# A mixture-of-experts stage on one Trainium2 core: other runs per weight load, a gather of four experts in rounded halves, a split scatter

## The chip, the cores and the metric

The kernel runs on one core of a Trainium2 chip. The core has a matrix engine (TensorE, PE, with its weight loads shown apart as PEld), a vector engine (VectorE, DVE), an engine for pointwise functions (ScalarE, ACT), a general engine (GpSimd, POOL) and a sync engine (SyncE, SP) that issues most of the transfers from memory. The metric is the device time of one execution in microseconds. Three runs of the kernel before took 1729.75, 1730.45 and 1731.28 us; the median is 1730.45.

## The reference

Two blocks of two layers each work on 256 tokens of 1024 numbers. Both layers of the second block end in a mixture of experts, and this is all that the change touches:

```python
def hierarchical_moe(x, w_group, b_group, w_expert, b_expert, w_gate, w_up, w_down):
    ...
    combine = jnp.sum(jax.nn.one_hot(expert_id, N_EXPERTS, dtype=jnp.float32) * top_w[..., None], axis=1).astype(t.dtype)
    y = jnp.zeros_like(t)
    for e in range(N_EXPERTS):
        hid = jax.nn.silu(t @ w_gate[e]) * (t @ w_up[e])
        y = y + combine[:, e:e + 1] * (hid @ w_down[e])
    return y.reshape(bsz, seq, dm)
```

There are 16 experts in 4 groups. A token takes one group and two experts of it. Gate and up are 1024 x 512, down is 512 x 1024, all fp32: 6 MiB per expert, 96 MiB per layer.

## The kernel before

Everything is computed in fp32 quality. Where fp32 operands are used as they are, one logical matmul leaves two records in the trace; where operands are rounded to fp32r, it leaves one.

**Weights.** `MoeQueue` (L52 to L112) lists a layer's loads in the order of use. Each is 1 MiB, [128 partitions, 4 x 512]: four rows of 2 KB for each partition, from four places in memory. SP issues a load as soon as a slot (a buffer of 8 KB per partition) is free. Slots come from two pools with 14 buffers, from a pool `mb` with two more that opens with the stage, and from buffers that the stage before no longer needs: `xl`, `nrm`, `g`, `xh`, each used once, and in the last layer `mk` and `mv`. That makes 20 in layer 0 and 22 in layer 1. The loads of a layer begin long before its stage, during the attention that comes ahead.

**Routing** (L1500 to L1580) takes one of two token tiles of 128 after the other: the logits, the two experts, the weights `C`, and for every token its place `pos` in its expert's list of up to 64.

**The loop** (L1640 ff.) takes the experts in eight pairs, q = 0 to 7; each expert of a pair has 64 columns of TensorE to itself, so the two experts' matmuls run side by side when they stand side by side in the instruction stream. The steps are: `select` (L1602, DVE) writes a 0/1 matrix for the pair; `gather` (L1613, PE) multiplies h with it, 16 fp32 matmuls of 128 columns, and the result xg is copied from two PSUM banks (L1615); gate and up (L1648, 32 logical matmuls); silu on ACT and the product on DVE, giving hid (L1653, L1654); `scatter` of the pair before (L1634, eight fp32r matmuls into four accumulators); `select_T` (L1621, L1623: sel turned, and the weights gathered); hid turned by four transposes (L1663) and copied to hT by DVE (L1665); the gather of the next pair; down (L1677, 16 logical matmuls into two banks, one half of the columns after the other); and Y, the down product scaled by the weights, as a rounded part and a rest (L1683 on ACT, L1684 on DVE).

**Overflow.** When an expert has more than 64 tokens, an arm `moe_dense` computes the rest. It stands inside the last pair's down product in the code (L1674), the branch is taken by a count that is loaded into registers (L1656), and its instructions lie in the stream of every engine: some 490 listed rows on PE. The given inputs don't need it.

**Order.** A list scheduler places each engine's instructions, so the order on an engine is not that of the code. PSUM has eight banks, four for the accumulators and four for all the rest.

Of the kernel before, what the change touches and what calls it, by code (L numbers as in the profile page):

```python
# [11 lines left out]
F32 = mybir.dt.float32  # L12
# [43 lines left out]
class MoeQueue:  # L56


    def __init__(self, nc, wq, wo, wg, wu, wd):
# [18 lines left out]
    def fetch(self, n=99):  # L78
        while n and self.free and len(self.loaded) < len(self.queue):
            ap, a = self.queue[len(self.loaded)]  # L80
            slot = self.free.pop(0)
            v, m = [], a // slot[3]
            for u in range(slot[3]):
                t = slot[0].tile([128, 2048 // slot[3]], F32, tag=slot[1], name="mw").rearrange("p (k f) -> p k f", k=m)
                self.nc.sync.dma_start(t, ap[:, u * m:u * m + m])
                v.append(t)
# [33 lines left out]
class Block:  # L120
# [227 lines left out]
    def layer_norm(self, x, mix, li, n, xh=None, xl=None, x32=None, alpha=ALPHA, after=None):  # L348
# [3 lines left out]
        for t in range(2):  # L352
# [1067 lines left out]
    def memattn(self, h, x, li, after=None):  # L1420
# [72 lines left out]
        self.layer_norm(h, acc, li, 1, x32=x32, after=after and (lambda t: after(x32, t)))  # L1493
        return x32

    def moe_prep(self, li, es):
# [9 lines left out]
        nc.scalar.dma_start(wr[:, :, 0:4], i["moe_w_group_2"][li].rearrange("(k p) g -> p k g", p=128), allow_slow_non_contiguous=True)  # L1506
        nc.scalar.dma_start(wr[:, :, 4:20], i["moe_w_expert_2"][li].rearrange("(k p) g -> p k g", p=128), allow_slow_non_contiguous=True)
# [72 lines left out]
    def moe(self, h, x32, r, li, last=False):  # L1580
# [5 lines left out]
        with ExitStack() as es:  # L1586
            mo = es.enter_context(tc.tile_pool(name="mo", bufs=1))
            mb = es.enter_context(tc.tile_pool(name="mb", bufs=self.extra))
# [3 lines left out]
            mq.add(mb, self.extra)  # L1592
            mq.once(self.xp, "xl")
            mq.once(self.gp, "nrm", 2)
            mq.once(self.gp, "g", 2)
            mq.once(self.xp, "xh")
            mq.fetch()

            def select(q):
                sel = mo.tile([128, 2, 128], F32, name="sel", bufs=2)  # L1600
                for t in range(2):
                    tt(sel[:, t].rearrange("p (e s) -> p e s", e=2), iota.unsqueeze(1).broadcast_to([128, 2, 64]),  # L1602
                       pos[:, t, 2 * q:2 * q + 2].unsqueeze(2).broadcast_to([128, 2, 64]), op=ALU.is_equal)
                return sel

            def gather(sel):
# [411 lines left out]
```

## Time and profile before

| | us |
|---|---|
| median of three runs | 1730.45 |
| profiled execution | 1729.29 |
| its span | 1727.2 |
| PE busy | 1622.4 |
| DVE busy | 827.7 |
| ACT busy | 651.4 |

The mean granted clock of PE in the profiled execution was 0.967 of full speed. The span is the time from the first to the last recorded instruction; all times in the rows count from its start. The expert stage of layer 0 runs from about 1046 to 1280, that of layer 1 from about 1483 to 1715. A step's cost on PE is best read from start to start: the ends of matmuls are modelled, and a row's length reaches into the next row. DMA windows give the bytes moved in a stretch, over its length.

### The profile page before, as it was taken

Reading aid. Unit: us, or ns where it says so; the run is one execution under the profiler, and the core shown is the slowest. Engines: PE = TensorE matmul, PEld = TensorE weight load, DVE = VectorE, ACT = ScalarE, POOL = GpSimd, SP = SyncE. Lnnn points to the kernel's source line nnn. Section 1 sums busy time; section 2 is a strip of 40 time slices with the busy share of each in tenths; the row PEclk is TensorE's granted clock in tenths of the full one; section 3 lists DMA queues with packets and bytes.
Section 4 is the critical chain, followed back from the end, with each engine's and each line's share of the span. In section 5 each row is a group of like instructions: output and inputs, shape, how many; then the busy total and the mean of one; then the engine's idle time right before and its main releaser. Section 6 shows DMA issues by size and latency. Waiting matters only on the chain. (4 is left out here: it accounts for less than half of the span.)

```text
span 1727.2 us, 25338 instructions
## 1 busy us (share of the span) xinstructions
PE 1622.4 (94%) x10127; PEld 1186.2 (69%) x10127; DVE 827.7 (48%) x1839; ACT 651.4 (38%) x1224; POOL 95.8 (6%) x98
## 2 busy tenths in 40 slices
PE   7899999989999999999999799999979989999995
PEld 6777999868767579999787775544337777544532
DVE  3566666475666257665666551111146865211112
ACT  5676455323244146554475431011026643101101
POOL 4610000001100000000101000000000000000000
PEclk9999999989899989999999899999989999899998
DMA  9334744323223556551943768999938286899993
GB/s 346 134 102 136 231 158 161 94 77 111 83 75 102 166 188 220 196 170 58 338 141 104 291 227 318 387 386 386 384 104 279 74 306 239 318 386 386 384 333 112
DMA packets 231373, 375.34 MB, mean 217 GB/s; under 512 B 17092, under 2 KB 105932, under 8 KB 231244
## 3 DMA queue, kind: packets, MB, share of 16 engines
q1 hardware_dynamic: 221360, 363.40, 59.9%
q10 hardware_dynamic: 9884, 10.19, 1.8%
q8 instruction: 84, 1.38, 0.3%
q14 instruction: 45, 0.37, 0.1%
HBM read 372.52 MB, written 1.05 MB: 216 GB/s over the span
## 5 line engine op out<-in xcount | busy, mean ns | idle before, releaser
L192 DVE TENSOR_TENSOR wl<-w,wh 128x1024 fp32r<-128x1024 f32 (+1 forms) x205 | 245.9, 1208 | 178.4 <-ACT wh L191 177.8
L191 ACT CAST wh<-w 128x1024 fp32r<-128x1024 f32 (+1 forms) x221 | 226.8, 1038 | 208.6 <-PE mm L216 125.7
L1648 PE MATMUL mm<-mw,xg 128*64 128x512 f32 x1024 | 230.2, 593 | 0.0
L215 PE MATMUL mm<-xh,wh 128*128 128x256 f32 x800 | 227.4, 284 | 0.4 <-ACT wh L191 0.4
L217 PE MATMUL mm<-xh,wl 128*128 128x256 f32 x800 | 227.4, 284 | 0.0
L216 PE MATMUL mm<-xl,wh 128*128 128x256 f32 x800 | 227.2, 284 | 0.0
L1648 PEld LDWEIGHTS mm<-mw,xg 128*64 128x64 f32 x1024 | 73.7, 137 | 144.0 <-issue 143.1
L215 PEld LDWEIGHTS mm<-xh,wh 128*128 128x128 f32 x800 | 152.3, 190 | 2.5 <-ACT wh L191 0.7
L216 PEld LDWEIGHTS mm<-xl,wh 128*128 128x128 f32 x800 | 151.8, 190 | 2.0
L217 PEld LDWEIGHTS mm<-xh,wl 128*128 128x128 f32 x800 | 151.9, 190 | 0.0
L1677 PE MATMUL mm<-mw,hT 128*64 128x512 f32 x512 | 118.7, 596 | 1.7 <-issue 1.7
L215 PE MATMUL acc<-wh,xh 128*128 128x512 f32 x284 | 113.7, 406 | 1.9 <-ACT xh L253 1.2
L216 PE MATMUL acc<-wl,xh 128*128 128x512 f32 x284 | 114.2, 403 | 0.0
L217 PE MATMUL acc<-wh,xl 128*128 128x512 f32 x284 | 113.6, 402 | 0.0
L1654 DVE TENSOR_TENSOR hid<-hid,mm 128x512 f32<-128x512 f32 x16 | 11.0, 688 | 168.3 <-PE mm L1648 168.3
L1677 PEld LDWEIGHTS mm<-mw,hT 128*64 128x64 f32 x512 | 36.6, 137 | 69.2 <-issue 67.1
L1684 DVE SCALAR_TENSOR_TENSOR Y<-mm,cs,Y 128x512 fp32r<-128x512 f32 x32 | 24.0, 751 | 114.2 <-ACT Y L1683 114.2
L1683 ACT ACTIVATE Y<-mm,cs 128x512 fp32r<-128x512 f32 x32 | 22.0, 687 | 147.0 <-PE mm L1677 147.0
L217 PE MATMUL acc<-wh,fl 128*128 128x512 f32 x176 | 69.8, 397 | 0.0
L215 PE MATMUL acc<-wh,fh 128*128 128x512 f32 x176 | 69.5, 395 | 0.0
L216 PE MATMUL acc<-wl,fh 128*128 128x512 f32 x176 | 69.3, 394 | 0.0
L1613 PE MATMUL mm<-sel,h 128*128 128x128 f32 x512 | 65.6, 290 | 0.5 <-DVE lg L1542 0.5
(511 smaller groups left out, 2814.0 us busy)
## 6 DMA issues: line engine op xcount, KB each, us to landing
mw<-in_moe_w_gate_dram SPq DMA_DIRECT2D x61, 1024.0 KB, 14.1
mw<-in_moe_w_up_dram SPq DMA_DIRECT2D x60, 1024.0 KB, 14.1
mw<-in_moe_w_down_dram SPq DMA_DIRECT2D x57, 1024.0 KB, 14.1
w<-in_ffn_w_gate_dram SPq DMA_DIRECT2D x22, 1024.0 KB, 6.6
w<-in_ffn_w_up_dram SPq DMA_DIRECT2D x22, 1024.0 KB, 5.5
w<-in_ffn_w_down_dram SPq DMA_DIRECT2D x22, 1024.0 KB, 5.1
w<-in_attn_w_qkv_dram SPq DMA_DIRECT2D x12, 1024.0 KB, 15.5
w<-in_rwkv_w_rkv_dram SPq DMA_DIRECT2D x24, 512.0 KB, 3.6
```

The source lines that it names most:

```text
L191: nc.scalar.copy(r[0], raw)
L192: (lo_eng or nc.vector).tensor_tensor(r[1], raw, r[0], op=ALU.subtract)
L215: mm(out, lhs[0], rhs[0], start=start, stop=False)
L216: mm(out, lhs[0], rhs[1], start=False, stop=False)
L217: mm(out, lhs[1], rhs[0], start=False, stop=stop)
L1613: mm(p[:, u * 128:u * 128 + 128], h[:, t, f * 128:f * 128 + 128], sel[:, t], start=t == 0, stop=t == 1)
L1648: mm(ps[64 * e:64 * e + 64], xg[:, k, e * 64:e * 64 + 64], mq.slab(w[2 * (k // 4) + e], k % 4), start=k == 0, stop=k == 7)
L1654: tt(hid, hid, gu[1], op=ALU.mult)
L1677: mm(pd[hf][64 * e:64 * e + 64], hT[:, k, 64 * e:64 * e + 64], mq.slab(w[2 * hf + e], k), start=k == 0, stop=k == 3)
L1683: act.activation(y[0], pd[hf], AF.Copy, scale=cs)
L1684: vec.scalar_tensor_tensor(y[1], pd[hf], cs, y[0], op0=ALU.mult, op1=ALU.subtract)
```

## The change

Five things change.

1. **Loads.** A load of gate or up gives each partition four neighbouring rows of the matrix, one run of 8 KB, in place of four of 2 KB. A load of down (but for the last pair's) takes 256 rows of 1024, two runs of 4 KB per partition, so one load now serves both halves of the columns for half of the inner dimension, and down goes over the inner dimension outside and the halves inside. The order of h's columns follows: the layer norm ahead of the stage writes h folded by 4, and the router's weights are read in the same order (four transfers in place of two).
2. **Gather.** h is split into a rounded part `hh` (ACT) and the rest `hl` (DVE), both fp32r, and one gather of 32 fp32r matmuls of 256 columns serves four experts: ahead of the loop (into the accumulators' banks) and at q = 1, 3 and 5 (into all four other banks).
3. **Buffers.** The pool `mb` is gone, `hl` lives in `xl`, and h's own buffer becomes a slot; h is put together again from its halves at q = 5. The slots go from 20 to 18 and from 22 to 20. sT gets two buffers, and Y's last tile one of its own.
4. **Scatter.** The first half of the scatter is written ahead of the turns, the second half behind them.
5. **Branch.** The If on the overflow prefers to fall through to the side without the arm.

```diff
-            for w in (wg, wu, wd):
+            for w in (wg, wu):
                 for c in range(2):
                     for e in (2 * p, 2 * p + 1):
-                        cut = w[e, :, c * 512:c * 512 + 512] if w is wd else w[e, c * 512:c * 512 + 512, :]
-                        self.queue.append((cut.rearrange("(k p) f -> p k f", p=128), 4))
+                        self.queue.append((w[e, c * 512:c * 512 + 512, :].rearrange("(p k) f -> p (k f)", k=4), 4))
+            for c in range(2):
+                for e in (2 * p, 2 * p + 1):
+                    if p == 7:
+                        self.queue.append((wd[e, :, c * 512:c * 512 + 512].rearrange("(k p) f -> p k f", p=128), 4))
+                    else:
+                        self.queue.append((wd[e, c * 256:c * 256 + 256, :].rearrange("(k p) f -> p k f", p=128), 2))
...
+                if len(ap.shape) == 2:
+                    self.nc.sync.dma_start(t, ap[:, u * n1:u * n1 + n1])
+                    v.append(t.rearrange("p (k f) -> p k f", k=m))
...
-                nc.vector.scalar_tensor_tensor(x[:, t, sl], sc[:, sl], st[:, 5:6], bb[:, sl], op0=ALU.mult, op1=ALU.add)
+                a, b = (v[:, sl].rearrange("p (q k) -> p k q", k=fold) for v in (sc, bb))
+                nc.vector.scalar_tensor_tensor(x[:, t, sl].rearrange("p (k q) -> p k q", k=fold), a, st[:, 5:6], b,
+                                               op0=ALU.mult, op1=ALU.add)
...
-            mb = es.enter_context(tc.tile_pool(name="mb", bufs=self.extra))
+            hh = mo.tile([128, 2, 1024], F32R, name="hh")
+            hl = self.xp.tile([128, 2, 1024], F32R, tag="xl", name="hl")
+            for t in range(2):
+                act.copy(hh[:, t], h[:, t])
+                tt(hl[:, t], h[:, t], hh[:, t], op=ALU.subtract)
             if last:
                 mq.once(self.mp, "mk")
                 mq.once(self.mp, "mv")
-            mq.add(mb, self.extra)
-            mq.once(self.xp, "xl")
             mq.once(self.gp, "nrm", 2)
             mq.once(self.gp, "g", 2)
             mq.once(self.xp, "xh")
+            mq.once(self.hp, "h")
...
-                sel = mo.tile([128, 2, 128], F32, name="sel", bufs=2)
+                sel = mo.tile([128, 2, 256], F32R, name="sel")
                 for t in range(2):
-                    tt(sel[:, t].rearrange("p (e s) -> p e s", e=2), iota.unsqueeze(1).broadcast_to([128, 2, 64]),
-                       pos[:, t, 2 * q:2 * q + 2].unsqueeze(2).broadcast_to([128, 2, 64]), op=ALU.is_equal)
+                    tt(sel[:, t].rearrange("p (e s) -> p e s", e=4), iota.unsqueeze(1).broadcast_to([128, 4, 64]),
+                       pos[:, t, 2 * q:2 * q + 4].unsqueeze(2).broadcast_to([128, 4, 64]), op=ALU.is_equal)
                 return sel
 
-            def gather(sel):
-                xg = mo.tile([128, 8, 128], F32, name="xg")
-                for g in range(2):
-                    p = self.ps()
-                    for u in range(4):
-                        f = 4 * g + u
-                        for t in range(2):
-                            mm(p[:, u * 128:u * 128 + 128], h[:, t, f * 128:f * 128 + 128], sel[:, t],
-                               start=t == 0, stop=t == 1)
-                    (act.copy, vec.tensor_copy)[g](xg[:, 4 * g:4 * g + 4], p.rearrange("p (u s) -> p u s", u=4))
+            def gather(sel, first=False):
+                xg = mo.tile([128, 8, 256], F32, name="xg")
+                ps = [(self.acc if first else self.ps)() for _ in range(4)]
+                parts = [(g, n) for n in range(4) for g in range(4)] if first else [(g, n) for g in range(4) for n in range(4)]
+                for g, n in parts:
+                    for u in range(2):
+                        f = 2 * g + u
+                        mm(ps[g][:, u * 256:u * 256 + 256], (hh, hl)[n % 2][:, n // 2, f * 128:f * 128 + 128], sel[:, n // 2],
+                           start=n == 0 and u == 0, stop=n == 3 and u == 1)
+                for g in range(4):
+                    (act.copy, vec.tensor_copy)[g % 2](xg[:, 2 * g:2 * g + 2], ps[g].rearrange("p (u s) -> p u s", u=2))
                 return xg
...
-                sT = mo.tile([128, 256], F32R, name="sT")
+                sT = mo.tile([128, 256], F32R, name="sT", bufs=2)
...
-                            mm(ps[64 * e:64 * e + 64], xg[:, k, e * 64:e * 64 + 64], mq.slab(w[2 * (k // 4) + e], k % 4),
+                            mm(ps[64 * e:64 * e + 64], xg[:, k, q % 2 * 128 + e * 64:q % 2 * 128 + e * 64 + 64], mq.slab(w[2 * (k // 4) + e], k % 4),
...
-                    for hf in range(2):
-                        scatter(q - 1, hf, *prev)
+                    scatter(q - 1, 0, *prev)
+                old = prev
                 sT, cs = select_T(q, sel)
                 p = self.ps()
                 for f in range(4):
-                    pe.transpose(p[:, f * 128:f * 128 + 128], hid[:, f * 128:f * 128 + 128], self.ident)
-                hT = mo.tile([128, 4, 128], F32, tag="hT", name="hT")
+                    turned = pe.transpose(p[:, f * 128:f * 128 + 128], hid[:, f * 128:f * 128 + 128], self.ident).ins
+                if old is not None:
+                    with tc.issue_after(turned):
+                        scatter(q - 1, 1, *old)
+                hT = mo.tile([128, 4, 128], F32, name="hT")
                 vec.tensor_copy(hT, p.rearrange("p (f s) -> p f s", f=4))
-                if q < 7:
+                if q % 2 and q < 7:
                     sel = select(q + 1)
                     xg = gather(sel)
+                if q == 5:
+                    h = self.hp.tile([128, 2, 1024], F32, tag="h", name="h")
+                    for t in range(2):
+                        nat, *parts = (v[:, t].rearrange("p (c a b) -> p c a b", c=2, a=a) for v, a in
+                                       ((h, 128), (hh.bitcast(F32), 4), (hl.bitcast(F32), 4)))
+                        tt(nat.rearrange("p c q k -> p c k q"), *parts, op=ALU.add)
                 w = mq.take(4)
                 pd = [self.ps(), self.ps()]
-                for hf in range(2):
-                    for k in range(4):
-                        if q == 7 and hf * 4 + k == 6:
-                            with tc.If(over > 64):
-                                self.moe_dense(mo, h, li, r["Co"])
-                        for e in range(2):
-                            mm(pd[hf][64 * e:64 * e + 64], hT[:, k, 64 * e:64 * e + 64], mq.slab(w[2 * hf + e], k),
-                               start=k == 0, stop=k == 3)
+                order = [(hf, k) for hf in range(2) for k in range(4)] if q == 7 else [(hf, k) for k in range(4) for hf in range(2)]
+                for n, (hf, k) in enumerate(order):
+                    if q == 7 and n == 6:
+                        with tc.If(over > 64, preferred_fallthrough_block=False):
+                            self.moe_dense(mo, h, li, r["Co"])
+                    for e in range(2):
+                        if q == 7:
+                            b = mq.slab(w[2 * hf + e], k)
+                        else:
+                            b = mq.slab(w[2 * (k // 2) + e], k % 2)[:, hf * 512:hf * 512 + 512]
+                        mm(pd[hf][64 * e:64 * e + 64], hT[:, k, 64 * e:64 * e + 64], b, start=k == 0, stop=k == 3)
                 mq.done(4)
                 Y = []
                 for hf in range(2):
-                    y = [mo.tile([128, 512], F32R, tag="hT" if hf and n else "Y%d%d" % (hf, n), name="Y") for n in range(2)]
+                    y = [mo.tile([128, 512], F32R, name="Y%d%d" % (hf, n)) for n in range(2)]
```

Three places in PE's order show what moves. The first is a middle pair, from the turn of sel to the first down matmul (acc are the scatter's accumulators, c_ident the identity that transposes are multiplied with). Before:

```order
L1621 MATMUL mm<-c_ident,sel 128x128 [waits PE_49]
L1621 MATMUL mm<-c_ident,sel 128x128
L1623 MATMUL mm<-C,sel 128x2 x2
L1663 MATMUL mm<-c_ident,hid 128x128 [waits DVE_49]
L1663 MATMUL mm<-c_ident,hid 128x128 x3
L1613 MATMUL mm<-sel,h 128x128 [waits Activation_49]
L1613 MATMUL mm<-sel,h 128x128 x7
L1613 MATMUL mm<-sel,h 128x128 [waits PE_49]
L1613 MATMUL mm<-sel,h 128x128 x7
L1677 MATMUL mm<-mw,hT 64x512 [waits DMAHW6_49,DVE_49,Activation_49]
```

After, in an even pair, where no gather follows:

```order
L1642 MATMUL mm<-c_ident,sel 128x128 [waits PE_49]
L1642 MATMUL mm<-c_ident,sel 128x128
L1644 MATMUL mm<-C,sel 128x2 x2
L1684 MATMUL mm<-c_ident,hid 128x128 [waits DVE_49]
L1684 MATMUL mm<-c_ident,hid 128x128 x3
L1655 MATMUL acc<-Y_10137,sT 128x512 [waits Activation_49]
L1655 MATMUL acc<-Y_10138,sT 128x512
L1655 MATMUL acc<-Y_10137,sT 128x512
L1655 MATMUL acc<-Y_10138,sT 128x512
L1711 MATMUL mm<-mw,hT 64x512 [waits DMAHW5_49,DVE_49,Activation_49]
```

The eight scatter matmuls stood ahead of these rows before; now four stand ahead and four between the turns of hid and the down product, where 16 gather matmuls stood.

The second place is late in layer 0, from the end of a down product into the next pair's gate matmuls. Before:

```order
L1677 MATMUL mm<-mw,hT 64x512 [waits DMAHW5_49,PE_49]
L1634 MATMUL acc<-Y,sT 128x512 [waits Activation_49]
L1634 MATMUL acc<-Y,sT 128x512
L1677 MATMUL mm<-mw,hT 64x512 [waits DMAHW6_49]
L1677 MATMUL mm<-mw,hT 64x512 x6
L1634 MATMUL acc<-Y,sT 128x512 [waits DVE_49]
L1634 MATMUL acc<-Y,sT 128x512
L1648 MATMUL mm<-mw,xg 64x512 [waits DMAHW7_49,PE_49]
L1634 MATMUL acc<-Y,sT 128x512 [waits Activation_49]
L1634 MATMUL acc<-Y,sT 128x512
L1634 MATMUL acc<-Y,sT 128x512 [waits DVE_49]
L1634 MATMUL acc<-Y,sT 128x512
```

After:

```order
L1711 MATMUL mm<-mw,hT 64x512 [waits DMAHW4_49]
L1711 MATMUL mm<-mw,hT 64x512 x5
L1655 MATMUL acc<-Y_10521,sT 128x512 [waits Activation_49]
L1655 MATMUL acc<-Y_10521,sT 128x512
L1655 MATMUL acc<-Y_10522,sT 128x512 [waits DVE_49]
L1655 MATMUL acc<-Y_10522,sT 128x512
L1669 MATMUL mm<-mw,xg 64x512 [waits DMAHW5_49,PE_49]
L1669 MATMUL mm<-mw,xg 64x512 [waits DMAHW6_49]
L1669 MATMUL mm<-mw,xg 64x512 x6
```

The first half of the scatter stands closed between the down product and gate, waiting for both parts of Y; before, it was spread over the down product and the first gate matmul.

The third is the branch at the layer's end. Before:

```order
L1634 MATMUL acc<-Y,sT 128x512 [waits Activation_49]
L1634 MATMUL acc<-Y,sT 128x512
L1656 TENSOR_LOAD cnti [waits DMAHW3_49,DMAHW4_49,DMAHW2_49,DMAHW5_49,DMAHW1_49,DMAHW6_49,DMAHW0_49,DMAHW7_49,DVE_49,Activation_49]
L1674 COMPARE_AND_BRANCH
L250 MATMUL mm<-c_ident,h 128x128 [waits PE_49]
```

After:

```order
L1655 MATMUL acc<-Y_12900,sT 128x512 [waits Activation_49]
L1655 MATMUL acc<-Y_12900,sT 128x512
L1677 TENSOR_LOAD cnti [waits DMAHW3_49,DMAHW4_49,DMAHW2_49,DMAHW5_49,DMAHW1_49,DMAHW6_49,DMAHW0_49,DMAHW7_49,DVE_49,Activation_49]
L1704 COMPARE_AND_BRANCH
L1704 UNCONDITIONAL_BRANCH [waits PE_49]
L260 MATMUL mm<-c_ident,h 128x128 [waits PE_49]
```

Behind the compare there stands now a plain branch, and the arm (from L260 in the second list, from L250 in the first) comes behind that.

## Rows read from the trace of the kernel before

**Rows 1.** The page's part 1: engine, busy time, share of the span, instructions.

```profile
PE 1622.4 (94%) x10127; PEld 1186.2 (69%) x10127; DVE 827.7 (48%) x1839; ACT 651.4 (38%) x1224; POOL 95.8 (6%) x98
```

**Rows 2.** Timeline of PE, one pair of experts: start, length, line, names, shape, count.

```profile
1099.33 13.90 PE L1648 MATMUL mm<-mw,xg 128*64 128x512 f32 x64
1113.16 2.13 PE L1634 MATMUL acc<-Y,sT 128*128 128x512 f32 x8
...
1115.71 0.63 PE L1663 MATMUL mm<-c_ident,hid 128*128 128x128 f32 x4
1116.18 3.74 PE L1613 MATMUL mm<-sel,h 128*128 128x128 f32 x32
1119.85 7.09 PE L1677 MATMUL mm<-mw,hT 128*64 128x512 f32 x32
```

**Rows 3.** Windows: stretch, length, busy time of five engines, clock, DMA share, GB/s.

```profile
1100.00:1200.00 100.00, 99.22 (x515) 45.49 (x512) 15.23 (x33) 10.07 (x18) 0.00 (x0) 1.00 1.05 386
822.00:826.00 4.00, 4.00 (x19) 3.23 (x18) 2.72 (x4) 2.44 (x6) 0.00 (x0) 1.00 1.02 413
172.00:174.00 2.00, 2.00 (x19) 2.00 (x18) 1.82 (x3) 1.08 (x2) 0.00 (x0) 1.00 1.08 351
1249.00:1254.00 5.00, 5.00 (x25) 1.51 (x22) 0.00 (x0) 0.00 (x0) 0.00 (x0) 1.00 0.96 357
1695.00:1700.00 5.00, 3.39 (x16) 1.24 (x14) 1.38 (x2) 0.00 (x0) 0.00 (x0) 1.00 0.00 0
```

**Rows 4.** Timeline of PE, second part of layer 1's last down product.

```profile
1705.27 3.65 PE L1677 MATMUL mm<-mw,hT 128*64 128x512 f32 x14
```

**Rows 5.** Timeline of PE, first and last of 27 matmuls of 256 columns.

```profile
39.78 0.28 PE L215 MATMUL acc<-xh,wh 128*128 128x256 f32 x1
...
42.87 0.28 PE L217 MATMUL acc<-xh,wl 128*128 128x256 f32 x1
```

**Rows 6.** Timeline of PE, the end of layer 0's first gather.

```profile
1039.88 6.16 PE L1613 MATMUL mm<-sel,h 128*128 128x128 f32 x28
```

**Rows 7.** Windows of layer 0: the first gather, two late stretches.

```profile
1040.00:1046.00 6.00, 6.00 (x31) 5.88 (x30) 0.54 (x4) 1.87 (x2) 0.00 (x0) 0.52 0.64 236
1181.60:1213.50 31.90, 31.11 (x152) 13.83 (x148) 4.34 (x9) 3.40 (x6) 0.00 (x0) 1.00 1.05 386
1213.50:1244.80 31.30, 30.52 (x148) 13.01 (x147) 3.88 (x7) 2.98 (x6) 0.00 (x0) 1.00 1.05 387
```

**Rows 8.** Timeline of DVE in layer 0's routing.

```profile
1028.45 0.21 DVE L366 TENSOR_SCALAR ln<-ln 128x1 f32<-128x1 f32 x1 [0.61 <-ACT acc L362]
...
1035.57 0.17 DVE L1560 SCALAR_TENSOR_TENSOR pos<-mm,M 128x16 f32<-128x16 f32 x1 [1.78 <-PE mm L1559]
...
1040.26 0.28 DVE L1602 TENSOR_TENSOR sel<-iota,pos 128x128 f32<-128x128 f32 x1
```

**Rows 9.** The page's part 5: busy us, mean ns, idle before and its releaser.

```profile
L192 DVE TENSOR_TENSOR wl<-w,wh 128x1024 fp32r<-128x1024 f32 (+1 forms) x205 | 245.9, 1208 | 178.4 <-ACT wh L191 177.8
...
L1684 DVE SCALAR_TENSOR_TENSOR Y<-mm,cs,Y 128x512 fp32r<-128x512 f32 x32 | 24.0, 751 | 114.2 <-ACT Y L1683 114.2
```

**Rows 10.** Timeline of PE, late in layer 0 and at its end.

```profile
1213.52 1.07 PE L1648 MATMUL mm<-mw,xg 128*64 128x512 f32 x2
1214.52 1.18 PE L1634 MATMUL acc<-Y,sT 128*128 128x512 f32 x4
...
1262.50 0.66 PE L1663 MATMUL mm<-c_ident,hid 128*128 128x128 f32 x4 [0.78 <-DVE hid L1654]
1263.98 4.48 PE L1677 MATMUL mm<-mw,hT 128*64 128x512 f32 x18 [0.83 <-issue]
...
1269.91 3.65 PE L1677 MATMUL mm<-mw,hT 128*64 128x512 f32 x14
1274.40 0.73 PE L1634 MATMUL acc<-Y,sT 128*128 128x512 f32 x2 [0.84 <-ACT Y L1683]
```

**Rows 11.** Line L1674 by operation: count, duration min/median/max ns, starts.

```profile
L1674 PEldq COMPARE_BRANCH  x2: 3706/3722/3739, 1275.5 to 1710.6; - x2
```

More of the change, by code (lines that the diff above doesn't have):

```diff
@@ L81, in fetch @@
             slot = self.free.pop(0)
-            v, m = [], a // slot[3]
+            v, m, n1 = [], a // slot[3], 2048 // slot[3]
             for u in range(slot[3]):
-                t = slot[0].tile([128, 2048 // slot[3]], F32, tag=slot[1], name="mw").rearrange("p (k f) -> p k f", k=m)
-                self.nc.sync.dma_start(t, ap[:, u * m:u * m + m])
-                v.append(t)
+                t = slot[0].tile([128, n1], F32, tag=slot[1], name="mw")
+                if len(ap.shape) == 2:
+                    self.nc.sync.dma_start(t, ap[:, u * n1:u * n1 + n1])
+                    v.append(t.rearrange("p (k f) -> p k f", k=m))
+                else:
+                    t = t.rearrange("p (k f) -> p k f", k=m)
+                    self.nc.sync.dma_start(t, ap[:, u * m:u * m + m])
+                    v.append(t)
             self.loaded.append(v[0] if slot[3] == 1 else v)
@@ L346, in store, with layer_norm @@
                 self.nc.sync.dma_start(out[t * 128:(t + 1) * 128, sl], h[:, t, sl])
-    def layer_norm(self, x, mix, li, n, xh=None, xl=None, x32=None, alpha=ALPHA, after=None):
+    def layer_norm(self, x, mix, li, n, xh=None, xl=None, x32=None, alpha=ALPHA, after=None, fold=1):
         nc = self.nc
@@ L1492, in memattn @@
         x32 = self.xp.tile([128, 8, 256], F32, tag="xh", name="x32")
-        self.layer_norm(h, acc, li, 1, x32=x32, after=after and (lambda t: after(x32, t)))
+        self.layer_norm(h, acc, li, 1, x32=x32, after=after and (lambda t: after(x32, t)), fold=4)
         return x32
@@ L1505, in moe_prep @@
         wr = one([128, 8, 20], "wr")
-        nc.scalar.dma_start(wr[:, :, 0:4], i["moe_w_group_2"][li].rearrange("(k p) g -> p k g", p=128), allow_slow_non_contiguous=True)
-        nc.scalar.dma_start(wr[:, :, 4:20], i["moe_w_expert_2"][li].rearrange("(k p) g -> p k g", p=128), allow_slow_non_contiguous=True)
+        for c in range(2):
+            nc.scalar.dma_start(wr[:, 4 * c:4 * c + 4, 0:4], i["moe_w_group_2"][li, c * 512:c * 512 + 512].rearrange("(p k) g -> p k g", k=4),
+                                allow_slow_non_contiguous=True)
+        for c in range(2):
+            nc.scalar.dma_start(wr[:, 4 * c:4 * c + 4, 4:20], i["moe_w_expert_2"][li, c * 512:c * 512 + 512].rearrange("(p k) g -> p k g", k=4),
+                                allow_slow_non_contiguous=True)
         br = one([128, 20], "br")
@@ L1619, in select_T @@
                 p = self.ps()
+                sel = sel.bitcast(F32)[:, :, q % 2 * 128:q % 2 * 128 + 128]
                 for t in range(2):
@@ L1634, in scatter @@
                         mm(acc[t][hf], sT[:, t * 128:t * 128 + 128], Y[hf][n], start=q == 0 and n == 0, stop=q == 7 and n == 1)
+            sel = select(0)
+            xg = gather(sel, True)
             acc = self.accs()
             stats = [self.small(8, "ln") for _ in range(2)]
-            sel = select(0)
-            xg = gather(sel)
             prev = None
@@ L1693, in moe @@
         self.layer_norm_both(h, acc, stats, li, 2, *(x or ()))
-        return x
+        return x, h
     def moe_dense(self, mo, h, li, Co):
@@ L1991, in build @@
                                 r["route"](x, t)
-                        x = b.moe(h, x, r, li, last=li == 1)
+                        x, h = b.moe(h, x, r, li, last=li == 1)
                     b.moe_queue = None
```

1 line of the change is left out of this document (added).

## The prediction

> **What bounds the kernel now.** I read the busy table first, then the order of time on TensorE (PE) inside the expert stage, then the DMA rates by window. PE is busy 1622.4 of 1727.2 us [rows 1], and in the expert stage nothing hides it: a middle pair of experts is one unbroken chain of PE work [rows 2]. The reader is to see there the starts, since each start less the next is what the step holds PE for: gate and up 13.83 us (1099.33 to 1113.16), scatter and the turn of sel 2.55, turns of hid 0.47, gather 3.67 (1116.18 to 1119.85), then the down product; the span repeats every 27.4 us. So a microsecond of PE work taken out here is a microsecond of the kernel, as long as the weights keep up.
>
> Do they? Twelve loads of 1 MiB (12.58 MB) per pair at 386 GB/s [rows 3] need 32.6 us against PE's 27.4, so the lead won before the stage is eaten. It suffices: in layer 1 the last load has landed at 1695, since nothing moves in the window from there [rows 3], and its part of the down product starts at 1705.27 [rows 4]. Some 10 us are left; in layer 0, where the stream still runs at 357 GB/s up to 1254 [rows 3] and the same piece starts at 1269.91 [rows 10], 16.
>
> **The gather.** Before, each of 8 gathers per layer costs 3.67 us (seven of them inside the loop, 25.7 us). After, 32 matmuls of 256 fp32r columns serve two pairs. That shape is in the trace elsewhere: 26 steps from 39.78 to 42.87 us, 0.119 us each, with a weight load of its own each time [rows 5]. 32 of them make 3.80 us, three inside the loop 11.4 us. Per layer −14.3 us, two layers **−28.6**. If the 0.119 didn't hold and each of them cost the 0.238 of half clock, the gain would be 2.9 per layer.
>
> [...] VectorE (DVE) gets two subtractions for hl of 1.21 us [rows 9]; one falls into an idle of 0.61 and pushes by 0.6, the other into one of 1.78 and costs nothing [rows 8]. The select on the path goes from 0.28 to about 0.5. Sum +0.5 per layer, **+1.0**; ends −2.5 and +4 per layer. The layer norm's last pass writes in folded order, a read with a stride of four words; no row shows one, so I bound it by nothing and by a doubling of a pass over 512 columns (0.75 by [rows 9]; four of them, 3.0, inside the +4), and take nothing.
>
> **The late pairs.** Near the end of a layer the list puts other work between the two experts' matmuls, which run side by side and lose that when they are parted. In before the stretches from gate start to gate start that hold two such places take 31.9 and 31.3 us instead of 27.4 [rows 7]. One parted matmul costs 1.00 us (1213.52 to 1214.52) instead of 13.83/32 = 0.43 [rows 10]; I take 0.45 for each half, 0.9 for a place. A gate/up product that ends straight in hid's turns idles 0.78 [rows 10]. Before, two late pairs in layer 0 pay three partings and the idle, 3.5 each, and one pays 1.7: 8.7, and the windows show 8.4 in excess. After, the scatter's first half stands right behind the down product in three of the last turns of each layer. The down product now ends both halves together, so Y's two passes are all still to come: the wait ahead of the scatter at the layer's end is 0.84, and DVE's second pass of 0.75 ends some 0.3 after the first two scatter matmuls [rows 9, 10], so 1.15. With one parting and the idle, 2.9; where gate's first matmul is put between, two partings, 3.4. Layer 0: 1.7 + 2.9 + 3.4 + 2.9 = 10.9, so +2.2; layer 1, by the same count of places, 2.9 + 3.4 + 3.4 = 9.7 against 3.4 + 3.5 before, +2.8. Together **+5.0**, with ends 0 (the excess stays) and +10.
>
> **Scatter on both sides of the turns.** hT's copy stands between hid's turns and the down product, 1.48 us from start to start with 0.83 idle [rows 10]. The gather covered it. In an even pair no gather is left, but scatter's second half (four matmuls, half of the 2.13 of eight [rows 2]) fills 0.47 + about 1.0 of the 1.48: nothing lost. Pair 0 has nothing to scatter: +0.85 per layer, **+1.7**. If the fill came too late in three even pairs, another 5.
>
> **The overflow arm.** PE's taken branch at the layer's end lasts 3706 to 3739 ns [rows 11], and the last scatter stands behind it. After, the compare falls through to a plain branch, but that has the same 490 rows of the arm to jump over: I take 0, with −4 per layer as the other end. [...]
>
> **The loads.** 4-KB runs moved 413 GB/s [rows 3]; no load of before shows 8-KB runs. I take 410 for both: 30.7 us per pair against the new mean of about 25.7 on PE. Two slots fewer put back the stream by up to two loads, 5.4 us; PE comes to the last load 11 us earlier. In layer 1 the 10 us of lead lose 16 and win about 11 to 12 (an estimate: the 74 loads left once the 20 slots and two refills are used, 77.6 MB, take 200.8 us at 386.5 and 189.3 at 410): 5 us of lead are left; cost 0, with ends 0 and the rival's 6. [...]
>
> h's rebuild at pair 5 (two DVE passes of 1.2 us or more) lies under the second half of gate/up, 6.9 us: 0.
>
> **Sum.** −28.6 + 1.0 + 5.0 + 1.7 = −20.9. The profiled execution took 1729.29 us, so 1708.4; the median of the runs is 1.2 above it, so 1709.5 in its terms.
>
> **The rivals.**
> Weights late: the longer runs bring no rate, 386.5 remains. For it speaks that 2-KB runs already fill the queues (share 1.05); against it the 413. Layer 0 keeps 16 − 11 = 5, less the slots 0; layer 1 ends 1 to 6 late. 1709.5 + 1 to 6: 1713.
>
> The arm really is out of the way and the compare falls through without a stall: 3.7 us per layer less; 1702. For it: the compare-branch is what carries the time; against it: the plain branch behind it.
>
> The stream slower than PE (the other side): 8-KB runs make the loads uneven, one run to one partition at a time, and PE waits in every pair. The slowest run length in the trace, 1 KB, moved 351 GB/s in its window [rows 3]. From about 370 GB/s on both layers wait so long (200.8 us becomes 209.8, twice, and 6 us of layer 1) that the gain is gone; at 351 it is 2 x 20.3 + 6, 1756. For it: slots are fewer and the lead is spent already; against it: every step to longer runs in the trace went up.
>
> The shorter gather doesn't come (0.238 each): 1709.5 + 22.8 = 1732, no change; against it the even steps of [rows 5].
>
> **How the numbers follow.** Forecast 0.55, weights late 0.15, no branch stall 0.17, stream too slow 0.08, no gather gain 0.05. The likeliest is 1709.5. Its own range is about 1700 to 1721: start −6 to +7, late pairs ±5, fill up to +5, not all at one end. The branch rival lies within it but for its lower part, down to 1698; the weights rival within it at the top. Range 1698 to 1722. A measurement of this kernel tells 0.2% (3.5 us) from no change: faster 0.87 (all but the last two rivals), same 0.05, slower 0.08.
>
> **What would show it.** The gather's rows at 0.119 each and three per layer inside the loop; even pairs near 23.8 us and odd ones near 27.6; PE idle of about 1.1 between down product and scatter in three late pairs; 0.85 idle in pair 0; a branch of 3 to 4 us on PE at the layer's end; 400 GB/s or more between 1060 and 1240; no wait of PE for a load. The forecast is wrong if PE's gate matmuls wait on DMA, if the windows stay at 386 and the last pairs stretch, or if the layer's start grows by more than 4 us.

## The result and the profile after

The changed kernel took 1705.14 us (median of 4 runs, 1703.31 to 1707.46), the kernel before 1730.1 in the same sessions. The ratio is 0.9861, 95% interval 0.985 to 0.9873. The prediction was 1709.5, between 1698 and 1722. The profiled execution of after took 1703.31 us, its span 1701.2.

Of the page of the kernel after, first PE's line of part 1 (busy time, share, instructions), then the transfer rates of the 40 slices:

```profile
PE 1588.7 (93%) x9871; PEld 1157.7 (68%) x9871; DVE 840.1 (49%) x1831; ACT 655.8 (39%) x1228; POOL 95.8 (6%) x98
...
GB/s 345 128 118 115 232 176 173 59 100 112 88 76 104 125 160 263 196 175 98 235 235 42 336 182 230 416 415 416 375 174 327 95 215 284 239 416 414 416 393 125
```

PE lost 33.7 us of busy time [rows 1] and the span 26.0. In the slices that lie wholly in the expert stages the stream now runs at 414 to 416 GB/s, where it ran at 386 to 387 [rows 3, 7].

Where the 26.0 us come from, by the starts of the first gate matmul of each pair and the last scatter matmul (profiled executions, us):

| stretch | before | after |
|---|---|---|
| up to layer 0's first gate | 1045.97 | 1045.66 |
| layer 0, pairs 0 to 7 | 25.9 27.4 27.4 27.4 27.5 31.9 31.3 35.2 = 234.0 | 23.5 27.7 24.1 27.7 27.8 28.7 33.2 34.1 = 226.7 |
| between the stages | 203.37 | 199.23 |
| layer 1, pairs 0 to 7 | 25.9 27.4 27.4 27.5 27.4 27.5 33.7 34.8 = 231.6 | 23.2 27.7 24.1 27.7 25.7 28.7 26.1 34.7 = 217.8 |
| after the last scatter | 12.3 | 11.8 |

Layer 0 won 7.3 us, layer 1 won 13.7. The 4.1 between the stages are mostly not the change's: runs below that share this part of the code took 202.5 to 204.1 there, and the profiled execution stands at the fast end of its four.

The timeline of PE after, pair 2 of layer 0, answers to [rows 2]: start, length, line, names, shape, count, idle before.

```profile
1096.80 13.90 PE L1669 MATMUL mm<-mw,xg 128*64 128x512 f32 x64
1110.63 1.20 PE L1655 MATMUL acc<-Y,sT 128*128 128x512 f32 x4
...
1112.25 0.63 PE L1684 MATMUL mm<-c_ident,hid 128*128 128x128 f32 x4
1112.64 1.16 PE L1655 MATMUL acc<-Y,sT 128*128 128x512 f32 x4
1113.98 7.09 PE L1711 MATMUL mm<-mw,hT 128*64 128x512 f32 x32 [0.18 <-issue]
1120.87 5.35 PE L1669 MATMUL mm<-mw,xg 128*64 128x512 f32 x24
```

No gather stands there; the scatter's second half (L1655 at 1112.64) fills nearly all of hT's copy, and 0.18 us stays idle. From gate to gate the pair takes 24.07 us. The gather of an odd pair, its first pair of matmuls, its last, and the down product behind it:

```profile
1617.83 0.40 PE L1632 MATMUL mm<-sel,hh 128*128 128x256 f32 x2
...
1621.39 0.40 PE L1632 MATMUL mm<-sel,hl 128*128 128x256 f32 x2
1621.72 7.09 PE L1711 MATMUL mm<-mw,hT 128*64 128x512 f32 x32
```

From 1617.83 to 1621.72 it holds PE for 3.89 us; from [rows 5] 3.80 was expected.

What cost most and was not expected is in pair 6 of layer 0. PE after:

```profile
1214.86 7.08 PE L1669 MATMUL mm<-mw,xg 128*64 128x512 f32 x30
1226.61 0.64 PE L1684 MATMUL mm<-c_ident,hid 128*128 128x128 f32 x4 [4.67 <-DVE hid L1675]
1226.99 1.97 PE L1655 MATMUL acc<-Y,sT 128*128 128x512 f32 x4
1228.89 7.92 PE L1711 MATMUL mm<-mw,hT 128*64 128x512 f32 x32
```

and DVE in the same time:

```profile
1215.37 0.32 DVE L1649 COPY cs<-mm 64x1 f32<-64x1 f32 x2 [8.57 <-ACT sT L1647]
1221.97 3.79 DVE L1698 TENSOR_TENSOR h<-hh,hl 128x1024 f32<-128x1024 f32 x2 [6.28 <-PE mm L1669]
1225.78 0.69 DVE L1675 TENSOR_TENSOR hid<-hid,mm 128x512 f32<-128x512 f32 x1
```

DVE's two passes that put h together again (L1698) wait 6.28 us for PE's gate/up and start when that has ended. hid's product (L1675) stands behind them in the queue, and PE waits 4.67 us for it. Then PE is slower for a while. Windows of after (stretch, length, five busy times, clock, DMA share, GB/s), with the stream's rate in the last:

```profile
1226.60:1229.00 2.40, 2.39 (x10) 1.56 (x12) 0.69 (x1) 0.00 (x0) 0.00 (x0) 0.60 0.99 403
1229.00:1233.00 4.00, 4.00 (x16) 1.26 (x17) 0.00 (x0) 0.00 (x0) 0.00 (x0) 0.81 1.01 424
1233.00:1237.00 4.00, 4.00 (x19) 1.58 (x17) 0.24 (x1) 0.78 (x2) 0.00 (x0) 1.00 1.00 424
...
1060.00:1200.00 140.00, 137.19 (x686) 62.91 (x686) 23.81 (x46) 15.62 (x27) 0.00 (x0) 1.00 1.02 416
```

Behind the idle the granted clock is 0.60 on average over 2.4 us and 0.81 over the next 4; from 1233 on it is 1.00 again.

In the other late pairs the wait for Y that the prediction counted did not come. At the end of pair 4 of layer 0, ACT and PE:

```profile
1174.17 0.69 ACT L1716 ACTIVATE Y<-mm,cs 128x512 fp32r<-128x512 f32 x1 [15.27 <-PE mm L1711]
1174.91 1.52 PE L1655 MATMUL acc<-Y,sT 128*128 128x512 f32 x4
```

ACT starts on the first half of the down product at 1174.17, ahead of PE's last two matmul records of the second half (1174.30 and 1174.35), and is done when the scatter can start. So the four scatter matmuls follow with no idle marked. They take 1.46 us from 1174.91 to the next gate matmul at 1176.37, where an early pair needs 1.04 for four.

The branch stands as it did [rows 10, 11], here in layer 1:

```profile
1684.34 0.74 PE L1655 MATMUL acc<-Y,sT 128*128 128x512 f32 x2 [0.84 <-ACT Y L1716]
1688.82 1.22 PE L1655 MATMUL acc<-Y,sT 128*128 128x512 f32 x2 [3.75 <-issue]
```

and PE's branches by operation (count, duration min/median/max ns, starts). The trace gives compares and plain branches one name; in order of time the two compares take 98 and 81 ns, and the plain branches behind them 3667 and 3300.

```profile
L1704 PEldq COMPARE_BRANCH  x4: 81/1699/3667, 1267.7 to 1685.5; - x4
```

And the layer norm's folded pass ahead of the router (L384), with the first subtraction for hl:

```profile
1023.49 2.22 DVE L384 SCALAR_TENSOR_TENSOR h<-nrm,ln,gb 128x512 f32<-128x512 f32 x2 [0.66 <-POOL ln L378]
...
1028.53 1.22 DVE L1608 TENSOR_TENSOR hl<-h,hh 128x1024 fp32r<-128x1024 f32 x1
```

Two folded passes take 2.22 us. Two plain ones took 1.41, here in the kernel before:

```profile
1023.45 1.41 DVE L373 SCALAR_TENSOR_TENSOR h<-nrm,ln,gb 128x512 f32<-128x512 f32 x2 [0.66 <-POOL ln L368]
```

### The profile page after: what moved, and what is told of

Same layout as the page of the kernel before. It is cut to its first block, busy times and chain, and to the rows that moved or that the text cites. A ratio compares the mean times of both kernels' runs of the same rounds, so it can differ in the third digit from the quotient of the medians.

```text
span 1701.2 us, 24789 instructions
## 1 busy us (share of the span) xinstructions
PE 1588.7 (93%) x9871; PEld 1157.7 (68%) x9871; DVE 840.1 (49%) x1831; ACT 655.8 (39%) x1228; POOL 95.8 (6%) x98
## 3 DMA queue, kind: packets, MB, share of 16 engines
HBM read 372.52 MB, written 1.05 MB: 220 GB/s over the span
## 5 line engine op out<-in xcount | busy, mean ns | idle before, releaser
L1669 PEld LDWEIGHTS mm<-mw,xg 128*64 128x64 f32 x1024 | 77.6, 137 | 140.6 <-issue 139.8
L1675 DVE TENSOR_TENSOR hid<-hid,mm 128x512 f32<-128x512 f32 x16 | 11.0, 688 | 147.2 <-PE mm L1669 147.2
L225 PEld LDWEIGHTS acc<-wh,xh 128*128 128x128 f32 x284 | 53.6, 189 | 14.9 <-ACT xh L263 1.6
```

Source lines behind the costliest of these rows:

```text
L225: mm(out, lhs[0], rhs[0], start=start, stop=False)
L1669: mm(ps[64 * e:64 * e + 64], xg[:, k, q % 2 * 128 + e * 64:q % 2 * 128 + e * 64 + 64], mq.slab(w[2 * (k // 4) + e], k % 4), start=k == 0, ...
L1675: tt(hid, hid, gu[1], op=ALU.mult)
```

## The experiments

All are edits of the changed kernel or of one another; times are medians of four runs (ten in one), ratios go against the kernel before on the same chip. Of the five parts the loads, the gather, the scatter and the branch were each put back or varied; the buffers (part 3) were not run by themselves, but for the rebuild of h.

**h rebuilt at the last pair.**

```diff
-                if q == 5:
+                if q == 7:
                     h = self.hp.tile([128, 2, 1024], F32, tag="h", name="h")
+                    with tc.issue_after(copied):
                     ...
```

(`copied` is hT's copy of the same pair.)

> The changed kernel, with h put together again at the last pair, behind the copy of hT, in place of pair 5. Theory: in layer 0 the two rebuild passes (3.8 us on DVE) wait for the slot that h's buffer had become, so they start only when pair 6's gate/up ends, and hid's product stands behind them; PE idles 4.67 us there where other late pairs idle 0.78. Moved, this stretch falls from 33.2 to about 29.3 us, layer 1 stays, and the kernel wins 3.9 us of 1705 (1701). Rival: DVE's passes hold up Y at the last pair instead (they need 3.9 us, and from hT's copy to Y there are 4.6), and the time stays the same; or the stall had another cause, and the 4.67 us remain.

1702.13 us (1699.35 to 1703.47), ratio 0.9843 (0.9827 to 0.986). Pair 6 of layer 0 fell from 33.18 to 27.74, layer 1 took 0.3 more. DVE at the last pair and PE at pair 6:

```profile
1251.90 0.69 DVE L1689 COPY hT<-mm 128x512 f32<-128x512 f32 x1 [0.75 <-PE mm L1684]
1252.51 3.94 DVE L1699 TENSOR_TENSOR h<-hh,hl 128x1024 f32<-128x1024 f32 x2
1257.20 0.75 DVE L1718 SCALAR_TENSOR_TENSOR Y<-mm,cs,Y 128x512 fp32r<-128x512 f32 x1 [0.75 <-ACT Y L1717]
```

```profile
1216.84 7.08 PE L1669 MATMUL mm<-mw,xg 128*64 128x512 f32 x30
1224.70 0.66 PE L1684 MATMUL mm<-c_ident,hid 128*128 128x128 f32 x4 [0.78 <-DVE hid L1675]
```

The passes fit between hT's copy and Y, and PE's idle is 0.78 again. The stall had the cause named. In its pair it cost 5.4 us, not 3.9: behind it, at the low clock (0.60, then 0.81), the scatter's second half and the down product take 1.90 and 7.89 us, here 1.10 and 7.11. The medians differ by 3.0 only, and the intervals of the two ratios overlap: the profiled execution of this run lost 5.3 us against that of after ahead of layer 0's first gate and between the stages, where the code is the same.

**Scatter's first half and the turn of sel kept behind gate/up.**

```diff
-                if prev is not None:
-                    scatter(q - 1, 0, *prev)
                 old = prev
-                sT, cs = select_T(q, sel)
+                with tc.issue_after(last_gu):
+                    if prev is not None:
+                        scatter(q - 1, 0, *prev)
+                    sT, cs = select_T(q, sel)
```

(`last_gu` is the pair's last gate/up matmul.)

> The changed kernel, with the first half of the scatter and the turn of sel kept behind the last gate/up matmul in every pair. Theory: what the late pairs lose (4 to 5 us each in layer 0 beside the rebuild, 1 to 2 in layer 1) comes from matmuls of the two experts parted from each other, a scatter that waits for Y right behind the down product, and hid's 0.78 us without cover; in this order all pairs before the last look like the early ones, 24.1 and 27.7 us. Gain 6 to 8 us in layer 0 and 4 to 5 in layer 1, 10 to 13 us in all (1693); the rebuild's stall of 3.9 stays. Rival: the other order only fills waits that are there anyway (for weights, for PSUM banks), and then PE idles at other places and the gain is under 3 us.

1690.43 us (1686.45 to 1692.85), ratio 0.9779 (0.976 to 0.9798). Layer 0's stage takes 217.5 instead of 226.7, layer 1's 211.8 instead of 217.8. PE in layer 0, pairs 6 and 7:

```profile
1212.96 0.51 PE L1644 MATMUL mm<-C,sel 128*128 128x2 f32 x4
1216.31 1.09 PE L1685 MATMUL mm<-c_ident,hid 128*128 128x128 f32 x4 [2.84 <-DVE hid L1675]
...
1227.54 13.95 PE L1669 MATMUL mm<-mw,xg 128*64 128x512 f32 x64
1241.42 1.19 PE L1655 MATMUL acc<-Y,sT 128*128 128x512 f32 x4
1242.45 0.38 PE L1642 MATMUL mm<-c_ident,sel 128*128 128x128 f32 x2
...
1243.03 0.63 PE L1685 MATMUL mm<-c_ident,hid 128*128 128x128 f32 x4
```

All pairs from 1 to 6 take 24.07 or 27.7, but for pair 6 of layer 0 (29.66), where the rebuild's stall is seen alone (2.84 idle). So some 15 us were lost to the order in which the scheduler put the late pairs, more than the 10 to 13 expected; by its gate-to-gate times the kernel before had 14.5 of the like.

**The loads as before.**

```diff
-            for w in (wg, wu):
+            for w in (wg, wu, wd):
...
-                        self.queue.append((w[e, c * 512:c * 512 + 512, :].rearrange("(p k) f -> p (k f)", k=4), 4))
+                        cut = w[e, :, c * 512:c * 512 + 512] if w is wd else w[e, c * 512:c * 512 + 512, :]
+                        self.queue.append((cut.rearrange("(k p) f -> p k f", p=128), 4))
```

(with the router's weights, the layer norm, h's rebuild and the down product's order to match)

> The changed kernel without its first part: loads of 2-KB runs, h not folded, down one half after the other. Theory: the stream falls from 415 to 386 GB/s; PE is about 11 us per layer faster than before the change and there are two slots fewer, so layer 1's last loads come 1 to 6 us late and PE waits for a load there, layer 0 hardly waits; the unfolded layer norm gives back 0.8 us per token tile, 1.6 per layer. Sum between -3 and +4 us against 1705. Rival one: the larger runs carry the gain (PE would wait in every late pair), and the time goes up by 10 us or more. Rival two: the stream never mattered and it is 3 us faster than the changed kernel.

1709.86 us (1706.04 to 1710.25), ratio 0.9887 (0.987 to 0.9903). The stream is back at 386 GB/s, and PE waits for loads at the last pair of layer 0, 0.86 and 1.62 us, and 1.64 at the same place of layer 1 (whose row names SP's queue as the releaser):

```profile
1100.00:1200.00 100.00, 97.39 (x480) 43.23 (x476) 14.69 (x29) 10.35 (x18) 0.00 (x0) 1.00 1.05 386
```

```profile
1246.72 3.78 PE L1660 MATMUL mm<-mw,xg 128*64 128x512 f32 x16 [0.86 <-DMA mw<-in_moe_w_up_dram]
1252.12 3.65 PE L1660 MATMUL mm<-mw,xg 128*64 128x512 f32 x14 [1.62 <-DMA mw<-in_moe_w_up_dram]
```

That is the mechanism of the rival "weights late"; it named layer 1 alone, and the time is 0.7 above the range expected here. With 2-KB runs the rest of the change would already have run into the stream. The 4.7 us against the changed kernel are not the price of the runs alone: the edit also takes back the order of the down product, the slow rebuild passes and the fold, and of the fold alone 1.6 per layer were expected back.

**A gather for two experts in every pair.**

```diff
-                sel = mo.tile([128, 2, 256], F32R, name="sel")
+                sel = mo.tile([128, 2, 128], F32R, name="sel", bufs=2)
...
-                if q % 2 and q < 7:
+                if q < 7:
```

> The changed kernel with a gather for two experts in every pair: 32 fp32r matmuls of 128 columns each, in place of 32 of 256 for four experts every second pair. Theory: what a gather costs is the number of its matmuls with a weight load of their own, about 0.11 us each whatever the columns, so seven gathers of about 3.6 us stand where three of 3.8 stood: +13.8 per layer, about 1731, the gain of the whole change gone. Rival: the cost goes by columns (0.06 each), and seven of 1.9 make 13.3 against 11.4: +2 per layer, about 1709.

1724.14 us (ten runs, 1713.99 to 1726.82), ratio 0.9959 (0.9943 to 0.9976). The first, second and last four of 32 matmuls, and the down product:

```profile
1117.23 0.56 PE L1632 MATMUL mm<-sel,hh 128*128 128x128 f32 x4
1117.63 0.61 PE L1632 MATMUL mm<-sel,hl 128*128 128x128 f32 x4
...
1120.31 0.61 PE L1632 MATMUL mm<-sel,hl 128*128 128x128 f32 x4
1120.84 1.08 PE L1711 MATMUL mm<-mw,hT 128*64 128x512 f32 x4
```

32 matmuls of 128 columns hold PE from 1117.23 to 1120.84, 0.113 each; with 256 columns it was 0.119. From 128 to 256 columns the cost goes by the count of matmuls, and all the gain of the gather is that each serves twice the columns: an early pair takes 27.38 here, 27.44 in the kernel before, and in the changed kernel 25.9 as the mean of 24.07 and 27.7. The sum came out 7 us below the 1731 expected, since this order has fewer late places (in layer 1 pairs 1 to 6 all take 27.38). Pair 6 of layer 0 goes the other way with 36.17: the rebuild's stall stands there ahead of a gather, and the gather runs at a granted clock of 0.50 until 1237.8.

**Both edits together** (rebuild and order).

> Both edits together: h rebuilt behind hT's copy at the last pair, and the scatter's first half and the turn of sel kept behind gate/up. Theory: the two stalls are separate; layer 0's pair 6, still 29.7 us with the order alone, goes to 24.1, so layer 0 takes about 212 us as layer 1 does, and the time is some 5.5 us under the 1690.4 of the order alone: 1685. Rival: with PE this fast the weights end late (PE waits for loads at the last pairs) and the 5.5 us turn into such waits: 1690.

1688.1 us (1686.58 to 1691.22), ratio 0.9771 (0.9755 to 0.9788). Pair 6 takes 24.07, but the last pair of layer 0 went from 33.4 to 36.1. In it PE waits ahead of the last quarter of gate/up:

```profile
1235.09 3.65 PE L1669 MATMUL mm<-mw,xg 128*64 128x512 f32 x14 [1.34 <-SPq L1706]
```

Of the 5.6 us in pair 6, 3.0 arrived in layer 0's stage and 2.3 in the medians; the rival had the rest. The wait goes with the weights of the last pair, which PE now asks for earlier. The row names SP's queue as the releaser, not a landing, but the transfers of this trace show that it was the stream: the last 8-KB packet of the loads of gate and up for layer 0 ends at 1234.60, 0.5 us before PE goes on. With the order alone that packet ends at 1235.03, and the quarter that needs it starts at 1237.84.

**Both halves of the scatter ahead of the turns, on top of both edits.**

```diff
-                        scatter(q - 1, 0, *prev)
+                        for hf in range(2):
+                            scatter(q - 1, hf, *prev)
...
-                if old is not None:
-                    with tc.issue_after(turned):
-                        scatter(q - 1, 1, *old)
```

> As the kernel with both edits, but with both halves of the scatter ahead of hid's turns, as before the change. Theory: in even pairs and in the last pair nothing stands any more between the turns and the down product while hT is copied, so PE idles 0.8 us there: four places per layer (pairs 2, 4, 6, 7), 6 to 7 us in all; even pairs go from 24.07 to 24.9. Rival: the copy comes earlier by as much, since hid is ready long before the turns (they would start behind eight scatter matmuls), and the difference is under 2 us.

1697.45 us (1694.98 to 1698.88), ratio 0.9818 (0.9802 to 0.9834): 9 us slower than with the halves parted, where 6 to 7 were expected. In the two stages of the profiled executions it is 7.1; most of the rest lies ahead of layer 0's first gate, where the code is the same. Even pairs take 24.99 instead of 24.07, and odd ones 28.05 instead of 27.7, which was not expected. An even pair's turns and down product:

```profile
1169.06 0.63 PE L1686 MATMUL mm<-c_ident,hid 128*128 128x128 f32 x4
1170.79 7.11 PE L1711 MATMUL mm<-mw,hT 128*64 128x512 f32 x32 [1.10 <-issue]
```

1.10 idle stands there in place of 0.18.

**Both edits with the loads as before.**

> As the kernel with both edits, but with the 2-KB runs of before and h not folded. Theory: PE asks for weights some 8 us per layer earlier than in the run with small loads that waited 2.5 and 1.6 us; at 386 GB/s the stream can't follow, and PE waits about 8 to 10 us more per layer on loads: 1698 to 1702 against 1685 (the unfolded layer norm gives 3 back). So the larger runs are what lets the other parts pay. Rival: the loads have more room than I count, PE waits as little as with small loads alone, and the time stays within 4 us of 1685.

1711.13 us (1707.26 to 1712.39), ratio 0.9897 (0.988 to 0.9913): 23 us slower than with the large runs, and 9 beyond the top of what was expected. Layer 0's last pair, four waits for loads in a row:

```profile
1233.60 3.77 PE L1660 MATMUL mm<-mw,xg 128*64 128x512 f32 x16 [1.19 <-DMA mw<-in_moe_w_gate_dram]
1239.01 3.85 PE L1660 MATMUL mm<-mw,xg 128*64 128x512 f32 x16 [1.64 <-DMA mw<-in_moe_w_gate_dram]
1244.43 3.80 PE L1660 MATMUL mm<-mw,xg 128*64 128x512 f32 x16 [1.58 <-DMA mw<-in_moe_w_up_dram]
1249.85 3.65 PE L1660 MATMUL mm<-mw,xg 128*64 128x512 f32 x14 [1.63 <-DMA mw<-in_moe_w_up_dram]
```

Each quarter of gate/up waits 1.2 to 1.6 us: PE runs at the stream's pace. The quarters start 5.4 us apart, and each needs two loads of 1 MiB, which makes 387 GB/s. The same two edits that win 17 us with large runs win nothing with small ones (1711.1 against 1709.9, with overlapping intervals).

**The fold moved out of the layer norm, on top of both edits.**

```diff
...
-                act.copy(hh[:, t], h[:, t])
+                hk = h[:, t].rearrange("p (c q k) -> p c k q", c=2, k=4)
+                act.copy(hh[:, t].rearrange("p (c k q) -> p c k q", c=2, k=4), hk)
```

> As the kernel with both edits, and with the folding moved out of the layer norm: h is written in its natural order (a pass over 512 columns at 0.70 in place of 1.11 us), and the copies that split h in halves read it folded; the router's weights are read as before. Theory: each token tile's path to the router is 0.8 us shorter, 1.6 per layer, about 3 us in all: 1682. Rival: the copies themselves get longer by the strided read (ACT's hh stands ahead of the copies of the turned h), and give it back: 1685 or more.

1688.91 us (1687.76 to 1692.7), ratio 0.9778 (0.9762 to 0.9794): no gain over 1688.1. By line, up to layer 0's first gate matmul (count, busy us, mean ns, idle before):

```profile
L1604 ACT CAST hh<-h 128x1024 fp32r<-128x1024 f32 x2 | 4.1, 2036 | 3.1 <-DVE h L366 3.1
...
L384 DVE SCALAR_TENSOR_TENSOR h<-nrm,ln,gb 128x512 f32<-128x512 f32 x4 | 2.8, 748 | 0.9 <-POOL ln L378 0.9
```

The layer norm's pass is back at 0.75 each, but ACT's copy of hh takes 2.04 where it took 1.05, and it stands ahead of the copies of the turned h, which start at 1024.92 as in the kernel with both edits. The rival held. The last pair of layer 0 adds to it: PE waits there for two loads, 1.00 and 1.36 us, and the pair takes 37.28 instead of 36.06.

**Without the arm.**

```diff
-                        with tc.If(over > 64, preferred_fallthrough_block=False):
-                            self.moe_dense(mo, h, li, r["Co"])
+                        pass
```

> The changed kernel without the overflow arm and its branch (tokens beyond 64 per expert would be left out; the given inputs have none). Theory: the arm's skip still costs what it cost before the change, in each layer PE's idle of 4.42 and 3.75 us ahead of the last scatter falls to below 1, and with it DVE's wait of about 3.3: 3.5 to 4 us per layer, 7 to 8 in all (1697). Rival: other waits (Y's second pass, the accumulators) stand right behind the branch, and under 3 us are won.

1699.95 us (1698.63 to 1701.02), ratio 0.9834 (0.9817 to 0.985). The last pairs take 29.5 and 30.7 instead of 34.1 and 34.7, 4.6 and 4.0 us less, though the medians differ by 5.2 only. The end of layer 0:

```profile
1265.80 1.52 PE L1655 MATMUL acc<-Y,sT 128*128 128x512 f32 x4 [0.84 <-ACT Y L1715]
```

All four last scatter matmuls run in one piece, 0.84 behind the down product. So skipping an arm that isn't needed costs 4.0 to 4.6 us per layer by the stage's rows. The kernel before was not run without its arm; its idle ahead of the last scatter, 4.26 and 4.03 us, is of the same size.

**The branch as before.**

```diff
-                        with tc.If(over > 64, preferred_fallthrough_block=False):
+                        with tc.If(over > 64):
```

> The changed kernel without its fifth part: the If falls through to the arm again, as before the change. Theory: one far jump per layer either way, PE's branch of 3.7 us only moves from the compare to the plain branch; the time stays within 2 us of 1705 and PE's idle ahead of the last scatter stays at 4 us. Rival: the plain branch is cheaper, and without part five each layer takes some 0.3 to 1 us more.

1706.76 us (1705.51 to 1708.47), ratio 0.9875 (0.9859 to 0.9892). PE ahead of the last scatter of layer 0:

```profile
1269.00 1.19 PE L1655 MATMUL acc<-Y,sT 128*128 128x512 f32 x2 [4.18 <-PEq L1704]
```

4.18 idle here, 4.42 in the kernel after and 4.26 before; the last pair 33.9 and 35.0 against 34.1 and 34.7. The compares, taken here, last 3632 and 3764 ns. Part five changes nothing that can be measured.

## Why the prediction was right, point by point

- **The gather** (−28.6): right. 3.89 us for four experts where twice 3.67 stood make −28.0, and the experiment with 128 columns shows why: a matmul costs 0.113 us there and 0.119 with 256, so the count of matmuls is what costs.
- **The first gather and the routing** (+1.0, ends −5 and +8): within its ends. From the turns of h to the first gate 20.39 and 18.34 us after, 20.73 and 20.54 before; in other runs of the same code 18.7 to 20.6. The 18.34 was at a granted clock of 1.00, the 20.39 at 0.85. No run shows the +0.5 per layer that the sum takes here: by these times it was −0.3 in layer 0 and −2.2 in layer 1, and the 16 matmuls of the gather's second half took 3.35 us in layer 0 at a granted clock of 0.57, 2.14 in layer 1 at 1.00. The folded pass was taken at nothing and costs 0.8 per token tile (1.41 to 2.22), inside the bound; in layer 0 the second half of the gather pays for it (1042.31 to 1045.66, where 1039.88 to 1045.97 stood [rows 6]).
- **The late pairs** (+5.0): the places were right, the size and the sign were not. Without the rebuild's stall, pairs 1 to 6 exceed the early ones by 8.4 us in layer 0 (8.3 before) and 4.6 in layer 1 (6.3 before): −1.5 in all, and the last pairs of the two layers fell by another 1.1. The wait of 1.15 for Y's two passes did not come: the down product does not end both halves together, ACT is done with the first half when the scatter starts, and its four matmuls take 1.46 us with no idle marked. Two partings with the scatter cost some 1.0 in pair 5 (28.67 against 27.7), where I had counted 1.8 and a wait. Nor did the windows confirm the 8.7 counted for the kernel before: their 8.4 is the excess of two pairs, the 8.7 a count over three.
- **h's rebuild** (0): wrong. I let it lie under gate/up, and had not asked what its destination waits for. It is a slot in use until the end of pair 6's gate/up in layer 0, and a pass takes 1.98 to 2.07 us, not 1.2. It cost 5.4 us in its pair. In layer 1 the slot came free ahead of hid and it cost nothing.
- **Scatter on both sides** (+1.7 in pair 0, nothing in even pairs): right in the main. Pair 0 has 0.83 idle and costs 2.2 in the two layers together; an even pair takes 24.07, where 27.44 less the gather's 3.67 is 23.77, so six of them cost 1.8 that the sum put at nothing. Without it 7.1 us are lost in the stages.
- **The arm** (0): right, as the run with the branch put back shows. On PE the plain branch lasts 3300 and 3667 ns, and the taken compare of that run 3632 and 3764. What the time goes into is not shown.
- **The loads** (0): right for this kernel. The rate came out at 416 (1060 to 1200), above the 410 taken. In the kernel after no matmul of the expert stages waited for a load, and two weight loads did, 0.3 us each.
- **The sum**: −20.9 forecast, −25 by the medians, −26.0 by the profiled executions. That it came so near is partly luck. In the two stages −21.9 was forecast and −21.0 measured, but layer 0 won 4 us less and layer 1 some 3 us more than forecast: the late pairs, 7.6 too dear, pay for the rebuild, 5.4 too cheap, and for the 2.3 of the scatter. Outside the stages +1.0 was forecast and −5.0 measured; 4.1 of it lie between the stages, where runs of the same code differ by as much.

## What to carry to other kernels

Ask of every instruction that writes a recycled buffer when that buffer comes free, and what stands behind it on its engine; a pass that is off the path gets onto it by its place in a queue. Where a matrix product loads its own weights each time, let each load serve more columns: here a matmul of 256 columns cost 0.119 us, one of 128 cost 0.113. When the weights' stream has little room, a faster engine soon wins nothing more: first the stream, then the order; here the same two edits were worth 17 us with large runs and nothing with small ones, and the version with both (1688.1) beats the kernel before by 2.3% and the changed one by about 1%.

## What the runs showed of the hardware

- The stream moved 386 GB/s with 2-KB runs (1100 to 1200 in two kernels) and 416 with runs of 4 and 8 KB mixed (1060 to 1200 in the kernel after).
- Two passes of DVE over 512 fp32 columns that read with a stride of four words take 2.22 us instead of 1.41, an ACT copy of 1024 columns 2.04 instead of 1.05.
- After 4.67 us without work PE was granted 0.60 of its clock on average over 2.4 us and 0.81 over the next 4, and a stall of 3.9 us more than usual cost 5.4.
- The stretch from the turns of h to the first gate took 18.3 us at a granted clock of 1.00, 18.7 and 19.8 at 0.91, and 20.3 to 20.6 at 0.83 to 0.85 in runs of the same code. Each kernel has one profiled execution, so whether this is what makes runs of one kernel differ is not shown.
